# Conditioning matmuls of a decoder layer in three bursts of six, six and four row tiles instead of four of four

## The chip, the core and the metric

The kernel runs on one core of a Trainium2 chip. The metric is the device time of one execution in microseconds. Before the change the median of three timed executions is 2013.61 us (2013.16 to 2013.98).

## What is computed

One layer of a conditioned decoder, for 256 prompt tokens and 8 x 8 sample tokens (320 token columns), with a width of 2048, all in float32. What matters here is the conditioning: a vector per sequence (one for the prompt, eight for the samples) goes through a large matrix and gives six sections of 2048 values that scale, shift and gate the layer's activations.

```python
mod = jax.nn.silu(c) @ w_ada + b_ada                      # w_ada: 2048 x 12288
sh1, sc1, g1, sh2, sc2, g2 = jnp.split(mod, 6, axis=-1)
h = _rmsnorm(x, norm1_g) * (1 + sc1) + sh1
p = h @ w_in                                              # q, k, v, gates, pooling input, ...
# gated linear attention and causal pooling, merged by sigmoid gates
x = x + g1 * (merged @ w_o)
h2 = _rmsnorm(x, norm2_g) * (1 + sc2) + sh2
gate, up = jnp.split(h2 @ w_gu, 2, axis=-1)
x = x + g2 * ((jax.nn.silu(gate) * up) @ w_down)
```

Sections 0 and 1 (sh1, sc1) are needed at once. Sections 4, 2, 3 and 5 (sc2, g1, sh2, g2) are needed later, and the change is about these four.

## The kernel before, in words

The large matrix products (`w_in`, `w_o`, `w_gu`, `w_down`) go by panels of 256 output columns. A panel runs through its contraction in chunks of four row tiles of 128: SyncE loads 512 KB (`raw_chunk`, line 135), ScalarE and VectorE split each weight into a high and a low part (`split`, line 147), and TensorE makes three matmuls per tile and half panel (`mm3`, lines 166 to 168). One chunk is 24 matmuls of 128x128 weights on 320 columns. Loaded chunks stand in a ring of three buffers.

The later sections of the conditioning are spread over this work. They are 64 blocks of 128 output columns, treated four blocks at a time: 16 groups, in the order of sections 4, 2, 3, 5. The contraction over 2048 is 16 row tiles per group. The weights of a group are eight pieces of two row tiles and 512 columns, 512 KB each, loaded by `ada_load` (line 241) into a ring of `AB = 3` buffers of their own. `ada_mm` (line 215) does one row tile: four matmuls, one for each block, placed at four column positions of the array, with the 32 conditioning columns as weights (128x32) and a block's 128 columns of `w_ada` as the moving operand. All row tiles of a group add up in one PSUM bank out of the four that `misc()` hands out (line 101), which the attention steps of the heads use too.

`ada_step` (line 248) does four row tiles, two pieces, in ascending order, and then asks for the next three pieces. With the fourth step of a group the sum is copied, transposed, and finished by `ada_out`. `ada_pump` (line 280) is called after every chunk of a large product; it adds a quarter of the set rate to a counter and calls a step when the counter reaches one. So a rate of 1.4 means 1.4 row tiles per chunk, 0.35 steps. The rate is set in three places: while heads 1 to 3 are projected (line 957: 116 chunks, of 9, 11 and 9 panels), in the `w_o` stage (line 1007, where after the sixth panel a loop issues whatever is missing), and in the gate and up products (line 1050). The limits 48 and 64 are the numbers of steps that must be done for three and for four sections.

The order of instructions on each engine isn't the program's own. A planner at build time arranges them by its own estimate of when each is ready; on the chip each engine then runs its list strictly in order and waits by semaphores. The first matmul of each row tile of the conditioning is kept behind the instruction traced before it on TensorE (`tc.keep_in_program_order`), so a burst doesn't move ahead of its place, but other work may be put between two row tiles. Loads of the conditioning and of the large products share SyncE's queue, and behind the head of the program their order is the planner's. In this text a burst is a run of conditioning matmuls with no other TensorE work between; a step is what one call of `ada_step` issues, and the planner may cut it into several bursts or join two.

Of the kernel before, what the change touches and what calls it, by code (L numbers as in the profile page):

```python
# [20 lines left out]
P = 128  # L21
# [4 lines left out]
KT = D // P  # L26
# [11 lines left out]
AB = 3  # L38
# [42 lines left out]
def body(tc, A):  # L81
# [15 lines left out]
    def nm(s):  # L97
        uid[0] += 1
        return "%s_%d" % (s, uid[0])

    def misc():
        return pmisc.tile([P, 512], F32, tag="m", name=nm("pm"))

    V, S, G, PE = nc.vector, nc.scalar, nc.gpsimd, nc.tensor
# [15 lines left out]
    scT = cp.tile([P, KT, 32], F32, name="scT")  # L120
# [6 lines left out]
    def tr(out, in_):  # L127
        k = in_.shape[0]
        PE.transpose(out, in_, ident[:k, :k])  # L129
# [40 lines left out]
    def proj(w, col, k0, k1, xh, xl):  # L170

        ps = pmain.tile([P, 2, 512], F32, tag="pm", name=nm("ps"))
        for c0 in range(k0, k1, 4):
            nk = min(4, k1 - c0)
            for j, whi, wlo in split_chunk(w[:, c0:c0 + nk, col:col + 256], nk, 256):
                kt = c0 + j
                for i in range(2):
                    mm3(ps[:, i, :T], whi[:, i * P:(i + 1) * P], wlo[:, i * P:(i + 1) * P],
                        xh[kt], xl[kt], kt == k0, kt == k1 - 1)
            ada_pump()  # L180
        return ps
# [30 lines left out]
    wgu = A["w_gu"][0].rearrange("(kt p) n -> p kt n", p=P)  # L212
    wdn = A["w_down"][0].rearrange("(kt p) n -> p kt n", p=P)

    def ada_mm(ps, k, raws, w):

        for j in range(4):
            ins = PE.matmul(ps[32 * j:32 * j + 32, 0:w], lhsT=scT[:, k, :], rhs=raws[j], start=k == 0,  # L218
                            stop=k == KT - 1, tile_position=(0, 32 * j))
            if j == 0:  # L220
                tc.keep_in_program_order(ins)

    def ada_out(dst, src, blk, shape):

        n = dst.shape[1]
        sec = blk // KT

        def wide(v):
            return v.rearrange("p (m c) -> p m c", m=shape[0]).unsqueeze(3).broadcast_to([P, *shape, 9])

        d4 = dst.rearrange("p (m c) r -> p m c r", m=shape[0])
        V.tensor_tensor(d4, src, wide(bada[:, blk:blk + n]), op=ALU.add)
        if sec in (1, 4):
            b0 = blk - sec * KT
            V.tensor_tensor(d4, d4, wide((N1G if sec == 1 else N2G)[:, b0:b0 + n]), op=ALU.mult)

    ada_q = [(s, b) for s in (4, 2, 3, 5) for b in range(0, KT, 4)]
    ada_raw = {}
    ada_ps = []

    def ada_load(c):

        if c < 8 * len(ada_q) and c not in ada_raw:
            sec, b = ada_q[c // 8]
            col = (sec * KT + b) * P
            ada_raw[c] = raw_chunk(wada[:, 2 * (c % 8):2 * (c % 8) + 2, col:col + 512], 2, 512, apool[0], "araw", AB)

    def ada_step():

        n = len(ada_done)  # L250
        sec, b = ada_q[n // 4]
        r = n % 4
        ada_done.append(n)
        for c in range(2 * n, 2 * n + 2):
            ada_load(c)
        if r == 0:
            ada_ps[:] = [misc()]
        ps = ada_ps[0]
        for j in range(4):
            raw = ada_raw[2 * n + j // 2]  # L260
            ada_mm(ps, 4 * r + j, [raw[:, j % 2, i * P:(i + 1) * P] for i in range(4)], P)
        for c in range(2 * n + 2, 2 * n + 2 + AB):
            ada_load(c)
        if r < 3:
            return
        sb = apool[0].tile([P, P], F32, tag="adasb", name=nm("adasb"))
        S.copy(sb, ps[:, 0:P])
        pt = misc()
        tr(pt[:, 0:P], sb)
        blk = sec * KT + b  # L270
        ada_out(mod[:, blk:blk + 4, :], pt[:, 0:P].rearrange("p (m c r) -> p m c r", m=4, c=1)[:, :, :, 0:9], blk, (4, 1))

    ada_done = []
    ada_acc = [0.0, 0.0, 0]

    def ada_rate(rate, limit):

        ada_acc[:] = [0.0, rate / 4, limit]

    def ada_pump():  # L280
        ada_acc[0] += ada_acc[1]
        if ada_acc[0] >= 1.0 and len(ada_done) < ada_acc[2]:
            ada_acc[0] -= 1.0
            ada_step()
# [4 lines left out]
    def mods(sec, kt):  # L289
        return mod[:, sec * KT + kt, 1:9].unsqueeze(2).broadcast_to([P, NB, LS])  # L290

    def s3(ap):
        return ap.rearrange("p (b t) -> p b t", t=LS)
# [81 lines left out]
    with tc.tile_pool(name="head", bufs=1) as xp:  # L375
# [29 lines left out]
        class HeadJob:  # L405
# [14 lines left out]
            def burst(self, k0):  # L420
                for ahead in range(3):
                    self.load(k0 + ahead * self.nk)
                raws = self.raws[k0]
                self.raws[k0] = None
                if self.ps is None:
                    self.ps = misc()
                w = self.w
                for i in range(self.nk):
                    ada_mm(self.ps, k0 + i, [raws[j // 2][:, i, (j % 2) * w:(j % 2) * w + w] for j in range(4)], w)
# [19 lines left out]
        for k in range(KT):  # L449
            pt = misc()  # L450
            for i in range(3):
                n = P if i < 2 else TS
# [17 lines left out]
        for i in range(3):  # L470
            n = P if i < 2 else TS
# [5 lines left out]
        for i in range(3):  # L477
            n = P if i < 2 else TS
# [50 lines left out]
        for si, (k0, k1) in enumerate(SLICES):  # L529
# [31 lines left out]
            while e < len(early):  # L561
                ge, kind, i, col = early[e]
# [391 lines left out]
            S.activation(merged[h], merged[h], AF.Sigmoid)  # L954
    queue += [sig0] + pst + st[:PSY] + psy + st[PSY:] + [merge_step(g0, E)]
    RATE = 10
    ada_rate(1.4, 48)
    for h in range(1, H):
        pump(RATE)
        g = new_group(h)  # L960
        for ui, (kind, i, col) in enumerate(units(h)):
# [5 lines left out]
            ps = proj(win, col, 0, KT, hh, hl)  # L967
# [22 lines left out]
    def sq_acc(acc, k, first):  # L990
        if first:
            S.activation(acc, x1[k], AF.Square)
        else:
            sq = fp.tile([P, T], F32, tag="sq", bufs=2, name=nm("sq"))
            S.activation(sq, x1[k], AF.Square)
            V.tensor_tensor(acc, acc, sq, op=ALU.add)

    def residual(ps, i, k, sec):
        V.scalar_tensor_tensor(x1[k][:, 0:TP], ps[:, i, 0:TP], modp(sec, k), x1[k][:, 0:TP],
                               op0=ALU.mult, op1=ALU.add)  # L1000
        t = fp.tile([P, TS], F32, tag="rt", bufs=2, name=nm("rt"))
        V.tensor_tensor(s3(t), s3(ps[:, i, TP:T]), mods(sec, k), op=ALU.mult)
        V.tensor_tensor(x1[k][:, TP:T], x1[k][:, TP:T], t, op=ALU.add)

    xs = fp.tile([P, KT, TS], F32, name="xs")
    tiny = fp.tile([P, 64], F32, name="tiny")[:, 0:1]
    ada_rate(1.6, 48)
    for ui in range(8):
        ps = proj(wo, 256 * ui, 0, KT, mh, ml)
        if ui == 5:  # L1010
            while len(ada_done) < 48:
                ada_step()
        for i in range(2):
            residual(ps, i, 2 * ui + i, 2)
            k = 2 * ui + i
            sq_acc(acc, k, k == 0)
            G.tensor_tensor(s3(xs[:, k]), s3(x1[k][:, TP:T]), mods(4, k), op=ALU.mult)
        if ui == 4:
            ada_rate(0, 0)
        if ui == 6:  # L1020
            S.activation(tiny, epst, AF.Sqrt)
# [25 lines left out]

    acc2 = fp.tile([P, T], F32, tag="acc", name="acc2")
    parts = ((0, 22), (22, 44))
    ada_rate(1.0, 64)  # L1050
    for pi, (f0, f1) in enumerate(parts):
        ah, al = {}, {}
        for f in range(f0, f1, 2):
# [20 lines left out]
        for ui in range(8):  # L1074
            ps = proj(wdn, 256 * ui, f0, f1, ah, al)
            for i in range(2):
                k = 2 * ui + i
                residual(ps, i, k, 5)
                if pi == 1:
# [4 lines left out]
                    for a in range(3):  # L1084
                        n = P if a < 2 else TS
                        tr(pt[:n, a * P:(a + 1) * P], xg[:, a * P:a * P + n])
                    for a in range(3):
                        n = P if a < 2 else TS
# [6 lines left out]
    for a in range(3):  # L1095
        n = P if a < 2 else TS
        PE.matmul(pt[:n, 2 * a:2 * a + 2], lhsT=acc2[:, a * P:a * P + n], rhs=ones[:, 0:2], start=True, stop=True)
    rr = fp.tile([P, 64], F32, name="rr")[:, 0:6]
    for a in range(3):
        n = P if a < 2 else TS  # L1100
# [3 lines left out]
    for a in range(3):  # L1104
        n = P if a < 2 else TS
# [30 lines left out]
```

## Time and profile before

| | |
|---|---|
| median of the timed executions | 2013.61 us |
| the profiled execution | 2011.32 us |
| its span on the core | 2009.5 us |
| granted TensorE clock, mean | 0.989 |
| TensorE matmul, busy | 1956.2 us, 97% |
| VectorE / ScalarE / GpSimd, busy | 1015.5 / 820.1 / 141.8 us |
| loads of `w_ada` | 192 of 512 KB, 5.8 us from issue to landing in the median |

The later sections run from 311 to 1285 us of the span. In the lists of instructions, a row gives the start in us, the duration in us, the engine, the line of the kernel, the operation, the tile written and the tiles read, and how many were merged into the row; a bracket at its end is the idle time of the engine before it, and what ended that. A TensorE matmul in float32 leaves two records, so a row tile of the conditioning is eight records and a step is 32. Windows are in us from the span's start.

### The profile page before, as it was taken

The page shows a single profiled execution, that of the slowest core. Times are in us where ns is not written, and L with a number is a line of the kernel's source. Part 1 is how long each engine was busy: PE and PEld are TensorE (multiplying, and loading weights), DVE is VectorE, ACT ScalarE, POOL GpSimd, SP SyncE. Part 2 cuts the span into 40 slices and gives each one's busy share as a digit, 9 for nine tenths or more (in the row PEclk, how much of TensorE's full clock was granted, in tenths as well). Part 3 has the DMA queues.
Part 4 walks back from the last instruction along what each step waited for, and adds up shares of the span by engine and source line. Part 5 has one row for each costly group of instructions (what it writes and reads, how often), then busy time and mean ns, then how long its engine had stood idle before and what let it go on. Part 6 is the DMA issues. An engine that isn't in the chain of part 4 may idle for free.

```text
span 2009.5 us, 37187 instructions
## 1 busy us (share of the span) xinstructions
PE 1956.2 (97%) x15008; PEld 1848.8 (92%) x15008; DVE 1015.5 (51%) x1881; ACT 820.1 (41%) x1466; POOL 141.8 (7%) x261
## 2 busy tenths in 40 slices
PE   7999999999999999999989999999999999999997
PEld 5789998888899899889979999999999999999997
DVE  3555665465546433665574444444444444444554
ACT  4333374354336333643344333343333344344443
POOL 1112220111001100110020000000000000000000
PEclk9999999999999999999989999999999999999998
DMA  9888754775975887569737666544444544444442
GB/s 301 285 302 272 234 155 147 253 255 186 314 237 167 281 263 229 156 230 340 234 105 223 206 205 203 168 148 154 145 152 149 155 149 147 151 154 144 150 142 91
DMA packets 319598, 400.83 MB, mean 199 GB/s; under 512 B 13529, under 2 KB 259801, under 8 KB 319089
## 3 DMA queue, kind: packets, MB, share of 16 engines
q1 hardware_dynamic: 307154, 358.21, 55.8%
q0 software_dynamic: 12272, 40.25, 5.7%
q8 instruction: 117, 1.92, 0.4%
q14 instruction: 55, 0.45, 0.1%
HBM read 373.96 MB, written 24.67 MB: 198 GB/s over the span
## 4 chain that ended last, share of the span: by engine, by line
PE 91%; DMA 5%; DVE 1%; ACT 1%; issue 1%; SPq 0%; POOL 0%; ACTq 0%; POOLq 0%; DVEq 0%
PE ps L166 27%; PE ps L168 26%; PE ps L167 26%; PE pm L218 5%; DMA raw<-w_in 2%; DMA raw<-w_ada 2%; PE pm L129 2%; PE pm L800 1%; PE pm L769 1%; PE pm L821 1%; DMA xn<-x_sample 1%; DVE wlo L153 0%; PE pm L796 0%; PE pm L758 0%; PE pm L641 0%
## 5 line engine op out<-in xcount | busy, mean ns | idle before, releaser
L153 DVE TENSOR_TENSOR wlo<-raw,whi 128x512 fp32r<-128x512 f32 x952 | 659.6, 697 | 834.0 <-ACT whi L152 827.2
L152 ACT CAST whi<-raw 128x512 fp32r<-128x512 f32 x952 | 587.0, 621 | 1013.4 <-PE ps L167 878.0
L166 PE MATMUL ps<-hh,whi 128*128 128x320 f32 x1408 | 445.9, 317 | 7.3 <-ACT whi L152 3.1
L166 PE MATMUL ps<-h2h,whi 128*128 128x320 f32 x1408 | 437.8, 311 | 5.1 <-ACT h2h L1042 5.1
L168 PE MATMUL ps<-hh,wlo 128*128 128x320 f32 x1408 | 441.6, 314 | 0.2 <-DVE wlo L153 0.2
L167 PE MATMUL ps<-hl,whi 128*128 128x320 f32 x1408 | 440.3, 313 | 0.3 <-DVE hl L495 0.3
L167 PE MATMUL ps<-h2l,whi 128*128 128x320 f32 x1408 | 435.5, 309 | 0.0
L168 PE MATMUL ps<-h2h,wlo 128*128 128x320 f32 x1408 | 435.5, 309 | 0.0
L166 PEld LDWEIGHTS ps<-hh,whi 128*128 128x128 f32 x1408 | 266.6, 189 | 30.8 <-issue 15.8
L168 PEld LDWEIGHTS ps<-hh,wlo 128*128 128x128 f32 x1408 | 266.6, 189 | 8.1 <-issue 6.1
L166 PEld LDWEIGHTS ps<-h2h,whi 128*128 128x128 f32 x1408 | 265.0, 188 | 9.3 <-ACT h2h L1042 6.1
L167 PEld LDWEIGHTS ps<-hl,whi 128*128 128x128 f32 x1408 | 266.9, 190 | 7.0 <-issue 5.4
L167 PEld LDWEIGHTS ps<-h2l,whi 128*128 128x128 f32 x1408 | 264.9, 188 | 0.0
L168 PEld LDWEIGHTS ps<-h2h,wlo 128*128 128x128 f32 x1408 | 264.9, 188 | 0.0
L166 PE MATMUL ps<-ah,whi 128*128 128x320 f32 x704 | 218.7, 311 | 0.0
L168 PE MATMUL ps<-ah,wlo 128*128 128x320 f32 x704 | 217.5, 309 | 0.0
L167 PE MATMUL ps<-al,whi 128*128 128x320 f32 x704 | 217.5, 309 | 0.0
L167 PEld LDWEIGHTS ps<-al,whi 128*128 128x128 f32 x704 | 132.2, 188 | 0.0
L166 PEld LDWEIGHTS ps<-ah,whi 128*128 128x128 f32 x704 | 132.2, 188 | 0.0
L168 PEld LDWEIGHTS ps<-ah,wlo 128*128 128x128 f32 x704 | 132.2, 188 | 0.0
L218 PE MATMUL pm<-raw,scT 128*32 128x128 f32 (+1 forms) x2688 | 109.9, 295 | 8.1 <-DMA raw<-w_ada 8.0
L218 PEld LDWEIGHTS pm<-raw,scT 128*32 128x32 f32 x2688 | 69.1, 111 | 36.0 <-issue 19.5
(279 smaller groups left out, 1542.6 us busy)
## 6 DMA issues: line engine op xcount, KB each, us to landing
raw<-w_ada SPq DMA_DIRECT2D x192, 512.0 KB, 5.8
raw<-w_gu SPq DMA_DIRECT2D x176, 512.0 KB, 3.5
raw<-w_in SPq DMA_DIRECT2D x173, 512.0 KB, 3.9
raw<-w_down SPq DMA_DIRECT2D x80, 512.0 KB, 3.3
S<-state_gla POOLq DMA_DIRECT2D x16, 1024.0 KB, 8.2
o_gs<-S POOLq DMA_DIRECT2D x16, 1024.0 KB, 5.9
raw<-w_o SPq DMA_DIRECT2D x32, 512.0 KB, 4.7
raw<-w_down SPq DMA_DIRECT2D x16, 256.0 KB, 2.6
```

The lines of the kernel that those rows point to most:

```text
L129: PE.transpose(out, in_, ident[:k, :k])
L152: S.copy(hi, raw)
L153: V.tensor_sub(lo, raw, hi.bitcast(F32))
L166: PE.matmul(ps, lhsT=whi, rhs=xhi, start=start, stop=False)
L167: PE.matmul(ps, lhsT=whi, rhs=xlo, start=False, stop=False)
L168: PE.matmul(ps, lhsT=wlo, rhs=xhi, start=False, stop=stop)
L218: ins = PE.matmul(ps[32 * j:32 * j + 32, 0:w], lhsT=scT[:, k, :], rhs=raws[j], start=k == 0, stop=k == KT - 1, tile_position=(0, 32 * j))
L769: PE.matmul(pt, lhsT=E["kdn"][:, s, d * P:(d + 1) * P], rhs=E["vn"][:, s], start=s == 0, stop=s == 1)
L800: PE.matmul(pt[32 * j:32 * j + 32, :], lhsT=qeP[:, d, 4 * gg + j, :], rhs=E["S0", gg, d][:, j], start=False, stop=d == 1, tile_position=(0 ...
L821: PE.matmul(pt, lhsT=kpz[:, gg, j, d * P:(d + 1) * P], rhs=E["vp"][:, gg], start=True, stop=True)
```

## The change

A step becomes a third of a group instead of a quarter. The first and the second step of a group take three pieces (six row tiles), the third takes two pieces (four row tiles). Within a step the pieces are taken in descending order, so the first matmul of a step reads the piece that was loaded last; the flags that open and close the PSUM sum go to the first and the last row tile as issued. After a step the next three pieces are asked for, as before. The number of steps falls from 64 to 48, and the rates and limits follow: 1.0, 1.4 and 0.75 instead of 1.4, 1.6 and 1.0 (a quarter of which is now a number of longer steps), and 36 and 48 instead of 48 and 64. What is loaded, multiplied and summed is the same.

```diff
-    def ada_mm(ps, k, raws, w):
+    def ada_mm(ps, k, raws, w, start=None, stop=None):
         for j in range(4):
-            ins = PE.matmul(ps[32 * j:32 * j + 32, 0:w], lhsT=scT[:, k, :], rhs=raws[j], start=k == 0,
-                            stop=k == KT - 1, tile_position=(0, 32 * j))
+            ins = PE.matmul(ps[32 * j:32 * j + 32, 0:w], lhsT=scT[:, k, :], rhs=raws[j],
+                            start=k == 0 if start is None else start, stop=k == KT - 1 if stop is None else stop,
+                            tile_position=(0, 32 * j))
...
     def ada_step():
         n = len(ada_done)
-        sec, b = ada_q[n // 4]
-        r = n % 4
+        sec, b = ada_q[n // 3]
+        r = n % 3
         ada_done.append(n)
-        for c in range(2 * n, 2 * n + 2):
+        c0 = 8 * (n // 3) + 3 * r
+        c1 = min(c0 + 3, 8 * (n // 3) + 8)
+        for c in range(c0, c1):
             ada_load(c)
         if r == 0:
             ada_ps[:] = [misc()]
         ps = ada_ps[0]
-        for j in range(4):
-            raw = ada_raw[2 * n + j // 2]
-            ada_mm(ps, 4 * r + j, [raw[:, j % 2, i * P:(i + 1) * P] for i in range(4)], P)
-        for c in range(2 * n + 2, 2 * n + 2 + AB):
+        todo = [(c, j) for c in reversed(range(c0, c1)) for j in range(2)]
+        for c, j in todo:
+            ada_mm(ps, 2 * (c % 8) + j, [ada_raw[c][:, j, i * P:(i + 1) * P] for i in range(4)], P,
+                   r == 0 and (c, j) == todo[0], r == 2 and (c, j) == todo[-1])
+        for c in range(c1, c1 + AB):
             ada_load(c)
-        if r < 3:
+        if r < 2:
             return
...
-    ada_rate(1.4, 48)
+    ada_rate(1.0, 36)
...
-    ada_rate(1.6, 48)
+    ada_rate(1.4, 36)
...
-            while len(ada_done) < 48:
+            while len(ada_done) < 36:
                 ada_step()
...
-    ada_rate(1.0, 64)
+    ada_rate(0.75, 48)
```

## The prediction

> **What bounds the kernel now.** I read the page first, then the stages by window, then the instructions around single conditioning bursts.
>
> ```profile
> span 2009.5 us, 37187 instructions
> PE 1956.2 (97%) x15008; PEld 1848.8 (92%) x15008; DVE 1015.5 (51%) x1881; ACT 820.1 (41%) x1466; POOL 141.8 (7%) x261
> ...
> PE 91%; DMA 5%; DVE 1%; ACT 1%; issue 1%; SPq 0%; POOL 0%; ACTq 0%; POOLq 0%; DVEq 0%
> PE ps L166 27%; PE ps L168 26%; PE ps L167 26%; PE pm L218 5%; DMA raw<-w_in 2%; DMA raw<-w_ada 2%; PE pm L129 2%; PE pm L800 1%; PE pm L769 1%; PE pm L821 1%; DMA xn<-x_sample 1%; DVE wlo L153 0%; PE pm L796 0%; PE pm L758 0%; PE pm L641 0%
> ...
> raw<-w_ada SPq DMA_DIRECT2D x192, 512.0 KB, 5.8
> ```
>
> TensorE is busy 97% of the span and makes 91% of the chain of waits, so TensorE time saved in a full stage is span saved. Line 218, the conditioning matmul, is 5% of the chain. The changed steps lie between 311 and 1285 us. The busy time by stage there (first the window, its length, then busy time per engine, granted clock, DMA share, GB/s):
>
> ```profile
> 436.00:508.00 72.00, 71.41 (x482) 62.20 (x482) 44.49 (x98) 36.62 (x77) 9.44 (x12) 1.00 0.55 177
> 508.00:604.00 96.00, 94.04 (x883) 86.44 (x885) 44.82 (x81) 30.14 (x51) 5.49 (x10) 0.98 0.85 277
> 682.00:813.00 131.00, 127.96 (x1209) 119.47 (x1207) 56.47 (x92) 44.29 (x72) 5.79 (x10) 0.99 0.81 261
> 896.00:985.00 89.00, 87.53 (x864) 80.45 (x866) 48.16 (x101) 31.89 (x59) 4.64 (x9) 1.00 0.90 306
> 1036.00:1290.00 254.00, 251.83 (x2087) 245.54 (x2088) 119.69 (x198) 102.87 (x183) 15.30 (x32) 0.99 0.62 194
> ```
>
> In all of them TensorE is the bound. In the second, third and fourth the DMA engines are near theirs too (0.81 to 0.90): there the conditioning, which a PSUM bank holds back while a head's attention runs (no burst between 436 and 508), catches up.
>
> **What one burst costs.** Three rows around each of three bursts, of 16, 32 and 48 records (a matmul leaves two records, a row tile is four matmuls, so 2, 4 and 6 row tiles):
>
> ```profile
> 404.28 0.31 PE L168 MATMUL ps<-hh,wlo 128*128 128x320 f32 x1
> 404.52 0.64 PE L218 MATMUL pm<-raw,scT 128*32 128x128 f32 x16
> 405.10 0.42 PE L166 MATMUL ps<-hh,whi 128*128 128x320 f32 x1
> 405.35 0.31 PE L167 MATMUL ps<-hl,whi 128*128 128x320 f32 x1
> ...
> 508.55 0.31 PE L168 MATMUL ps<-hh,wlo 128*128 128x320 f32 x1
> 508.79 1.52 PE L218 MATMUL pm<-raw,scT 128*32 128x128 f32 x48
> ...
> 510.49 0.31 PE L167 MATMUL ps<-hl,whi 128*128 128x320 f32 x1
> ...
> 1069.11 0.31 PE L168 MATMUL ps<-h2h,wlo 128*128 128x320 f32 x1
> 1069.35 1.08 PE L218 MATMUL pm<-raw,scT 128*32 128x128 f32 x32
> ...
> 1070.61 0.31 PE L167 MATMUL ps<-h2l,whi 128*128 128x320 f32 x1
> 1070.76 0.31 PE L168 MATMUL ps<-h2h,wlo 128*128 128x320 f32 x1
> ```
>
> From the start of the last ordinary matmul before a burst to the start of the second one after it there would be two ordinary spacings of 0.147 us (1070.61 to 1070.76, rounded), 0.29 us. It is 1.07, 1.94 and 1.50 us: a burst adds 0.78 us with 2 row tiles, 1.21 with 4, 1.65 with 6. Each two tiles are worth 0.435 us, and what is left, 0.34 us, is paid once per burst, however long it is: the switch to the 128x32 shape and back.
>
> **How many bursts.**
>
> ```profile
> L218 PE MATMUL pm<-raw,scT x2048: 272/273/423, 311.4 to 1284.5; 128*32 128x128 f32 x187
> ...
> 311.43 1.08 PE L218 MATMUL pm<-raw,scT 128*32 128x128 f32 x32
> ...
> 1283.70 1.08 PE L218 MATMUL pm<-raw,scT 128*32 128x128 f32 x32
> ```
>
> 2048 records are 64 steps of 32. In the timeline they stand as 84 separate bursts, from the first to the last row shown: many steps fall in two halves of 16, because the second piece was expected later and the planner put ordinary matmuls between.
>
> **The change part by part.**
>
> Fewer steps. Per group of four blocks, four bursts of 4 tiles (4 x 1.21 = 4.84) become two of 6 and one of 4 (2 x 1.65 + 1.21 = 4.51): 0.33 us less, times 16 groups, 5.3 us. All on the bounding engine. The 12 instead of 16 bursts of the gate/up stage (1036 to 1290) give 1.3 us of it, with no piece late there.
>
> Last piece first. A burst can no longer start on an early piece, so the planner has no reason to split it. 84 - 64 = 20 splits at 0.34 us. Four come from attention matmuls put between (around 337, 354 and 821), which the order of pieces doesn't touch; I leave these. 16 x 0.34 = 5.4 us. Bounds: 0, if the splits come back, and 6.8. Together -10.7 us.
>
> The same matmuls, DMAs, copies and transposes remain: 192 loads of w_ada with 128 of them here, 16 groups' ends. Vector and scalar work is unchanged.
>
> The wait. Before, a step took two of the ring's three buffers, and the third piece was already there; now a burst of 6 empties the ring. It waits for its third piece, and TensorE is in order: all ordinary matmuls queue behind it, then the copies of weights, whose buffers they free, then SyncE's loads of w_in behind those. Where it stands now:
>
> ```profile
> PE pm L218 <- DMA raw<-w_ada: 8.0, 4, 2.9
> ...
> 408.30 0.64 PE L218 MATMUL pm<-raw,scT 128*32 128x128 f32 x16 [1.62 <-DMA raw<-w_ada]
> 519.48 2.16 PE L218 MATMUL pm<-raw,scT 128*32 128x128 f32 x32 [1.94 <-DMA raw<-w_ada]
> 696.28 0.64 PE L218 MATMUL pm<-raw,scT 128*32 128x128 f32 x16 [2.94 <-DMA raw<-w_ada]
> 904.36 0.65 PE L218 MATMUL pm<-raw,scT 128*32 128x128 f32 x16 [1.47 <-DMA raw<-w_ada]
> 519.60:523.00 3.40, 3.38 (x37) 2.51 (x35) 0.00 (x0) 0.00 (x0) 0.76 (x1) 0.50 1.08 381
> 697.10:700.50 3.40, 3.40 (x14) 3.40 (x14) 0.60 (x1) 1.24 (x2) 0.00 (x0) 0.51 1.09 390
> 509.49 1.90 SPq L142 DMA_DIRECT2D raw<-w_ada  x3
> 683.30 3.12 SPq L142 DMA_DIRECT2D raw<-w_ada  x3
> ```
>
> Four stalls, 8.0 us, and after two of them the granted clock is 0.50 for 3.4 us, each worth 1.7 us: 11.4 us in all. Three of the four follow a burst of 48 records, that is, a refill of all three buffers at once, as after 508.79; this is what the change makes the rule. The third piece lands about 1.3 us behind the second (512 KB at the 381 to 390 GB/s of the rows). If the planner places the burst where it now places the second piece, each of the four waits 1.3 us longer, 5.2 us; if it has allowed for the extra piece, nothing. I take half, +2.6 us. Bounds: -11.4 (no stall left) and the rival below, every crowded burst late.
>
> The Trainium skill (TensorE: Matmul & The Clock Gate, Part 1) has the clock halve only after an idle window of about 3.4 us. By it none of these stalls costs clock, and they sum to 8.0 us. The trace disagrees: 0.50 from 519.60 on, after a gap of 1.94 us.
>
> Moved queue entries. On SyncE three w_ada loads instead of two now stand ahead of the next w_in or w_o load, 1.3 us more. The cover is the ring of three ordinary chunks, 24 matmuls x 0.147 = 3.5 us each, 10.6 us. If it is gone, the weight copies wait as they already do at seven places, without a TensorE gap put down to them, and I cost it at 0 (bounds 0 and 1.3 per burst in the crowded stretches, inside the rival's price):
>
> ```profile
> ACT whi L152 <- DMA raw<-w_in: 12.4, 4, 6.5
> ACT whi L152 <- DMA raw<-w_o: 11.4, 3, 6.6
> ```
>
> Rates. Counting chunks in the code, the 116 chunks of heads 1 to 3 now issue 29 bursts (156 row tiles) instead of 40 (160). In the w_o stage 0.35 per chunk, added in floating point, gives six of the missing seven by the fifth panel, and the loop after the sixth issues the last: some 15 us later than now (984), against a need at 1036. No cost. The ninth group, traced just before head 3's attention, starts at chunk 99 instead of 94 and holds its PSUM bank until 107 instead of 102; attention, from chunk 100, then has three banks instead of four for about 5 x 3.5 = 17.6 us longer. Cost between 0 and that; I take 0, because TensorE had ordinary matmuls to run through that whole stretch.
>
> Sum: -5.3 - 5.4 + 2.6 = -8.1 us. The profiled execution took 2011.32 us, 1.8 of it around the span; it would take 2003.2. It lies 2.3 us under the median of the timed runs, 2013.61; from that, 2005.5 us.
>
> **The rivals.**
>
> The stalls go too. With fewer, later bursts (every 4 chunks instead of 2.9) the pieces have longer to land: -10.7 - 11.4 = -22.1, 1991.5 us. For it: 60 of 64 steps already start without a stall. Against: refills of three are the ones that were late.
>
> Only the count falls. Splits return around attention matmuls, or the crowded stretches lose in TensorE gaps what they win in switches: -5.3 + 2.6 = -2.7, 2010.9 us. For it: in 896 to 985 the DMA engines run at 0.90, so moving switches may only move the wait. Also here: the change makes whole bursts, but the planner reorders everything else a little.
>
> Slower: in the crowded stretches (508 to 567, 682 to 742, 896 to 957) every burst waits for its own refill. Each holds 9 steps' worth of records (280 to 288 of line 218 by window, the last row below), so 6.75 bursts; about 17 in all follow another burst closely. At 2.0 us a stall (8.0/4) plus half of 1.7 for the clock, 2.85 us each, all 17 cost 48.5 us, 37 more than now: 2013.6 - 10.7 + 37 = 2040. It decides against the change from nine such bursts on (25.6 - 11.4 - 10.7 = +3.5), and with eleven it is 2023. For it: the ring has no spare piece any more. Against: between refills of one or two pieces the planner left ample room, as here, where the piece asked for at 527.93 was used at 539.92, 12 us later, without a gap, against 5.8 us to land:
>
> ```profile
> 527.93 0.37 SPq L142 DMA_DIRECT2D raw<-w_ada  x1
> 539.92 0.65 PE L218 MATMUL pm<-raw,scT 128*32 128x128 f32 x16
> ...
> 682.00:742.00 60.00, 10.98 (x288) 6.95 (x288) 0.97 0.90 302
> ```
>
> **How the numbers follow.** This kernel's measurement tells 0.2%, 4.0 us, from no change. The forecast, 2001 to 2009.5 around 2005.5, has a chance of 0.48; the stalls gone, under 2001, 0.10; only the count, 2009.6 to 2017.6, 0.22; slower, above that, 0.20. So faster 0.58, same 0.22, slower 0.20. The range takes half of the stalls-gone case and the lower half of the slower one: 1998 to 2021.
>
> **What would show it.** Between 311 and 1285 us, line 218 (its number shifts by one) stands as 48 to 52 bursts on TensorE, of 48 and 32 records, with 2048 in all; a burst of 48 adds 1.65 us. In the gate/up stage there are 12, and that stage is 1.3 us shorter. The waits of the conditioning matmul for w_ada are 8 to 14 us in four to six places, right behind the attention stretches. Many bursts of 16 would refute the second term; more than nine stalls in the crowded stretches, or a granted clock of 0.5 after several of them, would make the prediction wrong, as would a gap before the first w_o matmul near 898 us because attention ended late.

## The result, and the profile after

| | before | after |
|---|---|---|
| median of the timed executions, first job | 2013.8 us (2013.16 to 2014.08) | 1991.68 us (1990.94 to 1993.81) |
| the profiled execution, its span | 2011.32 us, 2009.5 us | 1993.81 us, 1992.0 us |
| bursts on TensorE in the later sections | 84 | 56 |
| TensorE idle in gaps over 0.15 us, 250 to 1400 us | 22.8 us | 19.0 us |
| of that, waiting for `w_ada` | 8.0 us | 4.3 us |
| granted clock at half, 250 to 1400 us | 27.3 us | 20.5 us |

The ratio is 0.9897, with an interval of 0.9883 to 0.9912. The kernel became faster by 1.0%, 22.1 us. The forecast was 8.1 us less, 2005.5, and its range ended at 1998, so the time lies outside. A second job on another chip gave 0.9899 (0.9877 to 0.9920), 2010.4 to 1992.46 us, 17.9 us less. The two profiled executions differ by 17.5 us: before's was 2.5 us under its median, after's 2.1 us over its own. Those 4.6 us are not in the two traces.

The page of the profile after, with the lines that answer to before's:

```profile
span 1992.0 us, 37175 instructions
PE 1942.7 (98%) x15008; PEld 1848.6 (93%) x15008; DVE 1014.1 (51%) x1881; ACT 819.6 (41%) x1468; POOL 137.5 (7%) x261
...
PE 93%; DMA 4%; DVE 1%; ACT 1%; issue 1%; SPq 0%; POOL 0%; ACTq 0%; POOLq 0%; DVEq 0%
PE ps L166 27%; PE ps L168 27%; PE ps L167 27%; PE pm L218 5%; PE pm L129 2%; DMA raw<-w_ada 1%; DMA raw<-w_in 1%; DMA raw<-w_o 1%; PE pm L804 1%; PE pm L825 1%; PE pm L773 1%; DMA xn<-x_sample 1%; PE pm L800 0%; PE pm L762 0%; DVE wlo L153 0%
```

TensorE is still the bound, with as many instructions and 13.5 us less busy time; transfers of `w_ada` fell from 2% to 1% of the chain. The same records of line 218 as before, and a burst of 48 in the gate and up stage with its neighbours:

```profile
L218 PE MATMUL pm<-raw,scT x2048: 272/273/422, 315.3 to 1267.3; 128*32 128x128 f32 x187
...
1064.24 0.31 PE L168 MATMUL ps<-h2h,wlo 128*128 128x320 f32 x1
1064.48 1.52 PE L218 MATMUL pm<-raw,scT 128*32 128x128 f32 x48
1065.93 0.42 PE L166 MATMUL ps<-h2h,whi 128*128 128x320 f32 x1
1066.18 0.31 PE L167 MATMUL ps<-h2l,whi 128*128 128x320 f32 x1
```

From 1064.24 to 1066.18 are 1.94 us; less the two ordinary spacings, 1.65, as forecast. The stalls for `w_ada` after the change, and the windows of the granted clock behind two of them (the clock is the third number from the end):

```profile
PE pm L218 <- DMA raw<-w_ada: 4.3, 3, 2.5
...
513.42 1.52 PE L218 MATMUL pm<-raw,scT 128*32 128x128 f32 x48 [1.36 <-DMA raw<-w_ada]
691.91 2.79 PE L218 MATMUL pm<-raw,scT 128*32 128x128 f32 x48 [2.53 <-DMA raw<-w_ada]
917.26 1.52 PE L218 MATMUL pm<-raw,scT 128*32 128x128 f32 x48 [0.39 <-DMA raw<-w_ada]
513.40:517.00 3.60, 3.58 (x62) 3.38 (x63) 1.29 (x2) 1.14 (x2) 0.00 (x0) 1.00 1.08 404
691.40:694.80 3.40, 2.89 (x49) 2.35 (x50) 0.98 (x2) 1.45 (x3) 0.00 (x0) 0.51 0.64 186
```

The first two stand where the forecast put them, at the first refill behind an attention stretch, but they are shorter than before; the third, of 0.39 us, is at the fourth burst behind such a stretch. Only the one of 2.53 us is followed by half clock. The other 3.4 us of half clock that went are at the first attention's psy matmul, which waits for ScalarE in both kernels, 3.38 us before and 2.21 us after. Before, two windows of half clock follow it, and after, one:

```profile
322.55 0.63 PE L166 MATMUL psy<-dh,whi 128*128 128x320 f32 x1 [3.38 <-ACT q L349]
321.60:325.00 3.40, 2.46 (x9) 2.46 (x10) 2.96 (x16) 1.33 (x2) 0.00 (x0) 0.50 0.02 5
325.00:328.40 3.40, 3.40 (x15) 3.40 (x14) 2.29 (x4) 0.62 (x1) 0.00 (x0) 0.50 0.43 117
```

```profile
322.18 0.41 PE L166 MATMUL psy<-dh,whi 128*128 128x320 f32 x1 [2.21 <-ACT q L353]
322.80:326.20 3.40, 3.40 (x17) 3.36 (x15) 2.94 (x12) 1.24 (x2) 0.00 (x0) 0.50 0.11 25
326.20:329.60 3.40, 3.40 (x27) 3.39 (x26) 2.41 (x6) 1.59 (x3) 0.00 (x0) 1.00 0.46 146
```

The quiet stage, the whole of the gate and up products, where nothing waits for `w_ada`, first before (16 bursts), then after (12):

```profile
1038.10:1834.30 796.20, 796.13 (x5798) 789.84 (x5799) 361.22 (x578) 311.66 (x518) 13.21 (x28) 1.00 0.53 164
```

```profile
1022.20:1817.00 794.80, 794.72 (x5798) 789.99 (x5799) 360.68 (x577) 311.43 (x518) 13.06 (x28) 1.00 0.52 165
```

It is 1.4 us shorter for four bursts less, 0.35 each.

### The profile page after: what moved, and what is told of

It reads as the page before. It is cut to its first block, busy times and chain, and to the rows that moved or that the text cites. A ratio compares the mean times of both kernels' runs of the same rounds, so it can differ in the third digit from the quotient of the medians.

```text
span 1992.0 us, 37175 instructions
## 1 busy us (share of the span) xinstructions
PE 1942.7 (98%) x15008; PEld 1848.6 (93%) x15008; DVE 1014.1 (51%) x1881; ACT 819.6 (41%) x1468; POOL 137.5 (7%) x261
## 4 chain that ended last, share of the span: by engine, by line
PE 93%; DMA 4%; DVE 1%; ACT 1%; issue 1%; SPq 0%; POOL 0%; ACTq 0%; POOLq 0%; DVEq 0%
PE ps L166 27%; PE ps L168 27%; PE ps L167 27%; PE pm L218 5%; PE pm L129 2%; DMA raw<-w_ada 1%; DMA raw<-w_in 1%; DMA raw<-w_o 1%; PE pm L804 1%; PE pm L825 1%; PE pm L773 1%; DMA xn<-x_sample 1%; PE pm L800 0%; PE pm L762 0%; DVE wlo L153 0%
## 5 line engine op out<-in xcount | busy, mean ns | idle before, releaser
L218 PE MATMUL pm<-raw,scT 128*32 128x128 f32 (+1 forms) x2688 | 104.7, 296 | 4.3 <-DMA raw<-w_ada 4.3
```

## The experiments

Theory: the time of these kernels is a constant, plus 0.335 us for every burst, plus TensorE's gaps, plus half of the time at half clock. Rivals: that the order of the pieces, the size of a step or the pace works on the waits in its own way; and that the gain beyond the bursts was the luck of one arrangement by the planner. The numbers of bursts are counted in the traces. Gaps and half clock are from the traces between 250 and 1400 us.

| kernel | bursts | gaps, of them `w_ada` | half clock | span | timed against before |
|---|---|---|---|---|---|
| before | 84 | 22.8, 8.0 | 27.3 | 2009.5 | 1 |
| after | 56 | 19.0, 4.3 | 20.5 | 1992.0 | 0.9897 (0.9883 to 0.9912) |
| after_again | 56 | 18.5, 5.2 | 17.1 | 1992.2 | 0.9899 (0.9877 to 0.9920) |
| order_only | 68 | 18.4, 4.2 | 17.1 | 1997.2 | 0.9945 (0.9930 to 0.9960) |
| three_ascending | 73 | 16.3, 1.1 | 13.7 | 1995.4 | 0.9932 (0.9913 to 0.9950) |
| pace_only | 81 | 23.3, 8.3 | 23.9 | 2004.6 | 0.9971 (0.9960 to 0.9982) |
| eight_of_two | 129 | 15.0, 2.2 | 13.7 | 2012.5 | 1.0031 (1.0018 to 1.0044) |
| after_old_pace | 48 | 16.3, 2.6 | 13.7 | 1989.4 | 0.9884 (0.9863 to 0.9904) |
| old_pace_again | 48 | 15.4, 2.2 | 17.1 | 1986.3 | 0.9877 (0.9864 to 0.9891) |
| ascending_old_pace | 71 | 20.7, 6.5 | 23.9 | 2001.1 | 0.9957 (0.9944 to 0.9969) |
| rate_102 | 51 | 20.0, 6.6 | 20.5 | 1992.9 | 0.9897 (0.9884 to 0.9911) |
| after_five_to_four | 53 | 22.5, 7.6 | 23.9 | 2004.1 | 0.9940 (0.9920 to 0.9960) |
| ring_of_four | 54 | 26.2, 5.0 | 20.5 | 2005.1 | 0.9938 (0.9915 to 0.9961) |
| two_of_eight | 36 | 20.0, 2.5 | 13.7 | 1987.0 | 0.9902 (0.9886 to 0.9917) |

Span less 0.335 us per burst, less the gaps, less half of the half clock, is 1942 to 1952 us in all fourteen, with a middle of 1947, while the spans run from 1986 to 2012. In each kernel 4.5 to 8.2 us of the half-clock time lie under gaps and are so counted twice at half weight; that is part of the constant. The three terms account for the differences to some 5 us. With the price of a burst left free, a straight line through the fourteen gives 0.30 us per burst.

**The order of the pieces alone.**

```diff
-        for j in range(4):
+        for j in (2, 3, 0, 1):
             raw = ada_raw[2 * n + j // 2]
-            ada_mm(ps, 4 * r + j, [...], P)
+            ada_mm(ps, 4 * r + j, [...], P,
+                   r == 0 and j == 2, r == 3 and j == 1)
```

The list of blocks stands as `[...]`, and `ada_mm` takes the two flags as in the change.

> Before's four steps of four row tiles at its own rates, with one edit: within a step the later piece is read first. The built list has 68 bursts in the later sections instead of 84 (after has 56). By the count of bursts alone (0.335 us each, from the spacing around bursts of before): 16 fewer, -5.4 us, 2008.4. If the order of the pieces is also what took the waits for w_ada and the clock they cost (some 11 to 13 us of the change's 22), it comes near 1996. If those went because of the size of the steps or of the pace, it stays at 2008.

0.9945: 11 us less (8 to 14), 2000.89 us against 2011.76. Sixteen bursts fewer are 5.4 of it. In the trace the gaps are 4.4 us less, and the time at half clock 10.2 less (5.1 us), so here too something beyond the count went: less than the expectation by the order had it, and not nothing. One of the three windows of half clock that went, the one at 281 us, stands in before behind a wait of 1.37 us that both kernels have, so it isn't the order's (see the last section). About half of the change's gain is in this one edit of the order.

**The three steps, in ascending order.**

```diff
-        todo = [(c, j) for c in reversed(range(c0, c1)) for j in range(2)]
+        todo = [(c, j) for c in range(c0, c1) for j in range(2)]
```

> After's three steps at after's rates, with the pieces read in ascending order. The built list has 73 bursts instead of after's 56. By the count alone 17 x 0.335 = 5.7 us above after, 1997.4, if the waits are as few as in after. If the order is what took the waits, they come back: 2008 to 2010. If a burst that starts on its first landed piece waits less, it would lie below 1997.

0.9932, against 0.9897 and 0.9899 of the changed kernel: 0.34% or 7 us slower, where the count says 5.7. The splits come back, as rows of 16 records show that in the changed kernel would be whole bursts:

```profile
535.79 0.64 PE L218 MATMUL pm<-raw,scT 128*32 128x128 f32 x16
536.71 0.65 PE L218 MATMUL pm<-raw,scT 128*32 128x128 f32 x16
540.67 0.65 PE L218 MATMUL pm<-raw,scT 128*32 128x128 f32 x16
...
PE pm L218 <- DMA raw<-w_ada: 1.1, 2, 1.0
```

The waits don't come back: 1.1 us, the fewest of all. So at this pace the waits are small without the descending order too.

**The pace alone.**

```diff
-    ada_rate(1.4, 48)
+    ada_rate(4 / 3, 48)
-    ada_rate(1.6, 48)
+    ada_rate(1.4 * 4 / 3, 48)
```

> Before's steps and order, with after's pace in row tiles per chunk (1.33 instead of 1.4 beside heads 1 to 3, 1.87 instead of 1.6 in the w_o stage). 81 bursts instead of 84: -1.0 us, 2012.8, by the count. If the slower pace is what ended the waits for w_ada, -12 more, near 2001.

0.9971, 6 us less (4 to 8), between the two expectations. The waits for `w_ada` stayed, 8.3 us. The pace is not what ended them. The three terms give 2.2 of the 4.9 us between the spans; where the rest comes from is open; it is within the 5 us to which the three terms account for differences.

**Steps of two row tiles.** One piece per step, eight steps per group, ring of three, rates and limits to match:

```diff
-        sec, b = ada_q[n // 3]
-        r = n % 3
+        sec, b = ada_q[n // 8]
+        r = n % 8
-        c0 = 8 * (n // 3) + 3 * r
-        c1 = min(c0 + 3, 8 * (n // 3) + 8)
+        c0, c1 = (8 * (n // 8) + (0, 1, 2, 3, 4, 5, 6, 7, 8)[r + e] for e in range(2))
...
```

> A step is one piece, two row tiles, eight steps per group, at after's pace in row tiles. 129 bursts, no step can be split by a late piece, and two pieces are always in reserve. If a burst costs 0.335 us whatever else happens: 73 more than after, +24.5 us, 2016.2, a little less where the few waits left in after (4.3 us) go too: 2011 to 2016. If the number of bursts does not matter, it comes out at after's 1992 or below, since its waits are the fewest.

1.0031 of before, 2017.76 us: 1.34% above the changed kernel's ratio, 27 us, for 73 bursts more (24.5 by the count). Its waits are few (2.2 us), and yet it is the slowest. The quiet stage, with 32 bursts:

```profile
1035.30:1836.50 801.20, 801.06 (x5796) 788.52 (x5797) 361.22 (x577) 311.99 (x517) 12.22 (x28) 1.00 0.52 163
```

801.2 against 796.2 with 16 and 794.8 with 12: 0.31 to 0.35 us per burst, with the same number of matmul records but for two, a mean granted clock of 1.00, and TensorE idle for 0.07 to 0.14 us. The price of a burst is shown here apart from every wait.

**The changed kernel at before's pace.**

```diff
-    ada_rate(1.0, 36)
+    ada_rate(1.05, 36)
-    ada_rate(1.4, 36)
+    ada_rate(1.2, 36)
```

> The changed kernel with the pace of before in row tiles per chunk (rates 1.05 and 1.2 instead of 1.0 and 1.4, that is 1.4 and 1.6 tiles per chunk). The built list has 48 bursts instead of 56. If bursts and waits are what the change is made of, 8 x 0.335 = 2.7 us below the changed kernel. If the slower pace beside the heads is what spares the waits, 5 to 8 us above it.

> after_old_pace once more (48 bursts), as the like of ascending_old_pace and to settle whether it beats the changed kernel: 0.988 of before by the first run, 0.9885 by the count from the changed kernel's 0.990.

The changed kernel beside the first of these on one chip:

> The changed kernel as it is, beside the other three of this job on one chip. 56 bursts. Both theories: 0.990 of before, 18 to 22 us less.

1989.31 us against 1992.46 for the changed kernel in that job; 0.9884, and 0.9877 in the second. 48 bursts, the least that three steps can have; 8 fewer are 2.7 us. The change's own pace did not help. Both ratios lie under the changed kernel's two, by 0.1 to 0.2%, but the intervals overlap, so that it beats the changed kernel is likely and not settled.

**The order again, at that pace.**

> after_old_pace with the pieces in ascending order: 71 bursts instead of 48. By the count 7.7 us above after_old_pace, 0.992 of before; with fewer waits for w_ada (1 to 3 us less), 0.991. If the order works in another way than through the count of bursts, no difference, or a larger one.

The edit is that of three_ascending on top of after_old_pace. 0.9957 against 0.9877 in the same job: 16 us, where 23 bursts are 7.7. Here the ascending order has more waits, not fewer, and two drops of the clock behind them:

```profile
516.51 1.08 PE L218 MATMUL pm<-raw,scT 128*32 128x128 f32 x16 [2.85 <-DMA raw<-w_ada]
517.52 0.64 PE L167 MATMUL ps<-hl,whi 128*128 128x320 f32 x1
517.95 0.47 PE L168 MATMUL ps<-hh,wlo 128*128 128x320 f32 x1
...
519.76 0.31 PE L166 MATMUL ps<-hh,whi 128*128 128x320 f32 x1
```

Behind the stall an ordinary matmul takes 0.47 instead of 0.31 us until 519.6. The gaps are 5.3 us longer than in old_pace_again and the half clock 6.8 (3.4 us), which with the 7.7 of the count covers the difference. With three_ascending's 1.1 us this says that the ascending order can go with many waits or few, depending on the arrangement; what in the arrangement decides isn't shown.

**A small shift of the rate.** `ada_rate(1.02, 36)` in place of `ada_rate(1.0, 36)`, nothing else.

> The changed kernel with a rate of 1.02 instead of 1.00 beside the heads: nothing but a small shift of where the planner puts things. 51 bursts instead of 56. By the count 1.7 us below the changed kernel, near 0.989 of before. If the change's gain beyond the count was the luck of one arrangement, this one can lie 5 us or more higher, 0.992 to 0.995.

0.9897, the changed kernel's own ratio, with 5 bursts fewer and 2.3 us more waiting for `w_ada`. So the gain isn't tied to one arrangement: this second one has it too. Of the 2.3 us of waits, 0.9 also lie between two executions of the changed kernel itself (4.3 and 5.2).

**A fourth buffer for the pieces.** It needs space, so the buffers of the split weights go from five to four in this kernel and in its like.

```diff
-WB = 5
-AB = 3
+WB = 4
+AB = 4
```

> The changed kernel with four instead of five buffers for the split weights (WB 4), as the like of the next one, which needs the space. 53 bursts. If the fifth buffer covers nothing now, 1 us below the changed kernel by the count; otherwise slower by what the splitting engines then make TensorE wait.

> The same with four instead of three buffers for the conditioning pieces: one piece stands in reserve when a burst of six tiles empties three. 54 bursts against 53. If the refill of an emptied ring is what the remaining waits for w_ada come from (4.3 us in the changed kernel, and the 3.4 us at half clock after one of them), 4 to 6 us below the one with WB 4 and a ring of three. If the waits come from the GLA transfers that fill the DMA queues at that time, no difference over 2 us.

The fifth buffer is worth 0.4%, 7 to 8 us: 0.9940 without it, against 0.9899 for the changed kernel in that job. With the spare piece 0.9938, no difference. The waits for `w_ada` in its trace are 5.0 instead of 7.6 us, but its other gaps are 6.3 us longer. The profiled executions of these two kernels were 6 to 7 us over their medians, so their rows in the table stand for long ones. A spare piece for the bursts made no difference to the time.

**Two steps of eight row tiles,** with that ring and those buffers:

```diff
-        c0 = 8 * (n // 3) + 3 * r
-        c1 = min(c0 + 3, 8 * (n // 3) + 8)
+        c0, c1 = (8 * (n // 2) + (0, 4, 8)[r + e] for e in range(2))
...
```

> Two steps of eight row tiles per group with a ring of four (and four buffers for the split weights, as in after_five_to_four), at the changed kernel's pace. The built list has 36 bursts against 53 there. If a burst costs 0.335 us: 5.7 us below after_five_to_four, 0.991 of before. If refilling four pieces at once brings waits, they take some of it back: 0.994 or more.

0.9902 against 0.9940: 7.6 us less for 17 bursts fewer (5.7), and not more waiting (2.5 us). A burst of 64 records:

```profile
1048.35 0.31 PE L168 MATMUL ps<-h2h,wlo 128*128 128x320 f32 x1
1048.59 1.95 PE L218 MATMUL pm<-raw,scT 128*32 128x128 f32 x64
1050.47 0.41 PE L166 MATMUL ps<-h2h,whi 128*128 128x320 f32 x1
1050.72 0.30 PE L167 MATMUL ps<-h2l,whi 128*128 128x320 f32 x1
```

2.37 us from 1048.35 to 1050.72, less 0.29, is 2.08; 0.34 and four times 0.435 make 2.08. The refill of four pieces at once took nothing back. With the fifth weight buffer it might be the fastest of all; no run had the space for both.

## Why the prediction was wrong

**What a burst costs** was right: 0.34 us each, whatever its length. It holds for 16 to 64 records, and in the quiet stage from 12 to 32 bursts.

**How many bursts** was nearly right. 56 instead of the 48 to 52 forecast; the rest are cuts by attention matmuls, eight instead of four. 28 x 0.335 = 9.4 us instead of 10.7.

**The wait** is the step that failed: "I take half, +2.6 us". It had the wrong sign. In the two traces the waits for `w_ada` went from 8.0 to 4.3 us. Of the half clock, one window behind such a wait went (519.60), and one behind the psy matmul, which the forecast had not counted, 1.7 us each: -7.1 instead of +2.6. With the bursts that is -16.5 of the 17.5 us between the spans.

The term stood on two views. The first was that a full refill of the ring is what makes a piece late. The trace after doesn't bear that out: 31 bursts of 48 records each empty the ring, and three bursts wait. What the record shows beside each of the four stalls before is that loads and stores of the attention's state (`state_gla` and `o_gs`, queue q0) took 48% to 65% of the DMA engines' time, and the loads of `w_ada` there took 7.4 to 10.6 us to land. First the 13 us up to the stall at 696.28, then a refill of three after the change that had no such neighbours and no stall (the window 713 to 723.7; the last number is the share of the 16 engines' time, or the median us from issue to landing):

```profile
q0 software_dynamic: 777, 3.05, 65.2%
raw<-w_ada SPq DMA_DIRECT2D x4, 512.0 KB, 9.7
```

```profile
q1 hardware_dynamic: 2272, 3.02, 85.6%
raw<-w_ada SPq DMA_DIRECT2D x3, 512.0 KB, 4.8
```

That these transfers are what makes the pieces late is argued from standing side by side; no run took them away. The second view was that the planner either leaves the burst where the second piece stood or allows for just one more transfer, 1.3 us. It allowed for more. Before and after, the three loads of a refill and the burst that waited for them:

```profile
509.49 1.90 SPq L142 DMA_DIRECT2D raw<-w_ada  x3
519.48 2.16 PE L218 MATMUL pm<-raw,scT 128*32 128x128 f32 x32 [1.94 <-DMA raw<-w_ada]
```

```profile
500.49 3.46 SPq L142 DMA_DIRECT2D raw<-w_ada  x3
513.42 1.52 PE L218 MATMUL pm<-raw,scT 128*32 128x128 f32 x48 [1.36 <-DMA raw<-w_ada]
674.73 3.11 SPq L142 DMA_DIRECT2D raw<-w_ada  x3
```

The last of the three issues ends at 511.4 before and at 503.95 after. Without the stall TensorE would have come to the burst at 517.5 and at 512.1: 6.2 us later before, 8.1 after. At the next head it was 6.9 (693.3 from 686.4) before and is 11.5 (689.4 from 677.8) now. At the first of these heads the burst before was already waiting for the first of its three pieces (issued at 509.49, landed 9.9 us later), not for the second, and after for the third. Counted from the first issue, TensorE would have come 3.5 us later than before, and the piece that it needed landed 2.9 us later. A burst that opens on its last piece stands later in TensorE's list, and ordinary matmuls fill the time.

That is how the waits went in this pair. What sets their size in general stays open: over the twelve further runs they go from 1.1 to 8.3 us, descending order had more of them than ascending at one pace and fewer at another, and a rate 2% higher moved them by 2.3 us. Of the 22.1 us, 9.4 are the bursts, shown by the quiet stage and by eight_of_two; 7.1 are waits and clock in the traces, not tied to one part of the change; 4.6 lie between the profiled and the timed executions; and 1.0 is not accounted for. Part of the 7.1 is luck: the changed kernel's own two traces differ by one window of half clock (20.5 and 17.1 us), 1.7 us.

**The rivals.** "The stalls go too" named 1991.5 us and had a chance of 0.10. Its number was hit by luck; its mechanism held only in part: more than half of its 11.4 us is still there (4.3 us of waits and one window of half clock, 1.7), and the psy matmul's window and the 4.6 us outside the traces made up for it. Nor do the runs bear out the reason it gave, fewer and later bursts: pace_only, with a step every 3 chunks instead of 2.9, kept its 8.3 us, and eight_of_two, with one every 1.5 chunks, had 2.2. "Only the count falls" is refuted, as the splits went. "Slower" is refuted: three bursts wait, not nine, and two_of_eight, which empties a ring of four, waits for two.

**Moved queue entries** cost TensorE little, as forecast: its gaps other than those for `w_ada` are 14.8 us before and 14.7 after. The weight copies do wait longer for loads, 32.0 us against 12.4, with TensorE's gaps at the start of the w_o stage under 1 us each:

```profile
ACT whi L152 <- DMA raw<-w_in: 32.0, 11, 7.4
ACT whi L152 <- DMA raw<-w_o: 12.7, 5, 9.8
```

**The rates** were costed at nothing. That was wrong by a little: at before's pace the same three steps need 48 bursts instead of 56, since none of its steps is cut.

**The range** was too narrow on the fast side. It took in half of the case without stalls, and that case's chance was set by the view that a full refill is what makes a piece late; four rows were all that this view stood on.

## What to carry to other kernels

When a stream of small matmuls of another shape is woven into a large product, price it by the burst: measure the spacing from the last ordinary matmul before it to the second after it, at two lengths, and take the part that doesn't grow. Then count the bursts in the trace, not the steps in the code, because a planner such as this one cuts a step where one of its inputs is expected later; opening the step on its last input keeps it whole, but for cuts by other work (eight here). When a load is late, look at what else the DMA engines carry at that time before you blame the load's own queue. Forecast waits that depend on a planner's placement with a range of both signs as wide as the waits themselves.

## What the runs showed of the hardware that I had not expected

A stall can cost the clock well before it has lasted as long as the drop itself, 3.4 us, and not every stall does: a gap of 1.94 us was followed by half clock before, one of 2.53 us after, and those of 1.36 us (above) and 1.62 us were not. The price of a stall has a part of 1.7 us that comes or doesn't.

Where the stall falls decides at least part of that. In each of the fourteen traces, half clock between 250 and 1400 us starts only at whole steps of 3.413 us from its first start there (before: 280.63, then 12, 70, 122 and 220 steps later). A wait of 1.37 us near 280 us stands in twelve of the traces: in seven it lies inside one step, and half clock follows in all seven; in five the border of two steps cuts it, and it follows in none. The changed kernel's two traces show the same at the second head, first after, then after_again:

```profile
688.03:691.44 3.41, 1.35 (x10) 1.08 (x8) 0.00 (x0) 0.00 (x0) 0.00 (x0) 1.00 1.06 388
```

```profile
693.01 1.52 PE L218 MATMUL pm<-raw,scT 128*32 128x128 f32 x48 [2.19 <-DMA raw<-w_ada]
688.47:691.88 3.41, 2.34 (x16) 2.08 (x15) 0.00 (x0) 0.00 (x0) 0.00 (x0) 1.00 1.05 384
691.88:695.30 3.42, 2.29 (x54) 2.09 (x55) 0.37 (x1) 1.02 (x2) 0.00 (x0) 1.00 0.82 261
695.30:698.71 3.41, 3.41 (x26) 3.41 (x25) 2.59 (x5) 1.89 (x4) 0.00 (x0) 1.00 1.00 371
```

In after 2.06 us of the stall's 2.53 lie in one step, and half clock follows from 691.44 on; in after_again the border at 691.88 cuts 2.19 us into two idle parts of about 1.1, and the clock stays at 1.00. How much idle time a step takes isn't settled by these traces: 1.37 us was enough near 280 us, and 1.36 to 1.62 were not at the stalls for `w_ada`.

One and the same kernel shows the effect between executions: in the job of after_again the kernel before took 2008.4 to 2010.4 us in the five executions with a mean granted clock of 0.990 or 0.991, and 2014.7 to 2016.6 us in the three with 0.988 or 0.989. 0.003 of 2010 us is 6 us, about the whole difference.
